# Gating and pooled products behind their pair's sixth product, the first output block out of its PSUM bank, SiLU as one ScalarE function

## The chip, the cores and the metric

The kernel runs on one core of one Trainium2 chip. The metric is device microseconds of one execution of the whole program, taken as the median of several runs; lower is better. A profile is one further execution, seen by the hardware profiler. Its engines are called PE (TensorE, the matmuls), DVE (VectorE), ACT (ScalarE), POOL (GpSimd) and SP (SyncE, which here issues most DMAs).

## The reference

One decoder layer on a sequence of 1024 tokens with 1024 channels, all in float32. One input projection feeds three token mixers and three gates:

```python
h = _rmsnorm(x, norm_g)
p = h @ w_in
(u, v, z_a, x_b, b_g, c_g, z_b, x_c, z_c, g_a, g_b, g_c) = jnp.split(p, ...)
# A: chunked spatial gating: u * (w_s . layernorm(gelu(v)) + b_s), u = gelu(u)
y_a = (_gmlp_branch(u, v, ln_g, ln_b, w_s, b_s) * jax.nn.silu(z_a)) @ w_pa
# B: gated causal convolution of width 3
y_b = (_shortconv_branch(x_b, b_g, c_g, conv_w, conv_b) * jax.nn.silu(z_b)) @ w_pb
# C: causal means over 2, 4, 8 or 16 tokens, minus x_c, times a 128 x 128 matrix per group
y_c = (_pool_branch(x_c, w_pool, pool_scale) * jax.nn.silu(z_c)) @ w_pc
merged = sigmoid(g_a) * y_a + sigmoid(g_b) * y_b + sigmoid(g_c) * y_c
out = _rmsnorm(x + merged @ w_o, final_g)
```

## The kernel before

**Stages.** First h is normalised, transposed and split into a high and a low half (a float32 product is made of three matmuls, `mm3`: high x high, high x low, low x high). v is projected by tokens and stored to DRAM. Then comes the long stage that the change touches, the input projection of everything else, and after it the branch projections (`py`, L699) and the output projection (`po`).

**Pairs.** The input projection walks over 28 `pairs` of 128-channel weight tiles (the loop at L497). Each pair has a kind: `g` (two gate tiles, Sigmoid), `a` (u and z_a), `b` and `bz` (the four tiles of mixer B), `c` (x_c and z_c). The first ten are g g g a g a g a g a; then b and bz take turns four times, then c and g four times, then two g. A pair's two output tiles, `o0` and `o1` (128 x 1024 each), are made by Strassen's scheme in Winograd's form: seven products of half size give four blocks. In the order of the code they are A11, A12, S2, S3, S1, A22, S4 (`PRODUCTS`, named by the left factor; PE rows in the profile carry these names). From the third pair on, A12's product is made for two neighbouring pairs together, ahead of the first of them, by cutting it once more into seven small products (`joint`); its result waits in SBUF as `p2`. So a pair then has six products of its own: A11, S2, S3, S1, A22, S4; A22 is the one that the title calls the sixth, S4 the last.

**Where a product goes.** Each product is one PSUM bank of 128 x 512 (`bank`, eight of them). ACT copies A11's to `s1`; DVE adds the others to running sums `u2` and `u3`, and `block` makes an output block of a bank and a sum and puts the pair's function on it. Weight tiles are combined on POOL (`T_n`, `T_j`), rounded on ACT (`ch`, `cj`) and their low halves made on DVE (`cl`), six products ahead (`AHEAD`).

**What an `a` pair adds.** In the `g` pair before it, `spatial` loads the mixer's weights and v (`vr`, 512 KB, from DRAM, on SP's queue) and `spatial_norm` normalises v: eight DVE instructions on `vr` (L425), two POOL multiplies and adds, an ACT rounding to `vh` and a DVE low half `vl`. `spatial_mm` (six matmuls into two banks, named `sg` in PE rows) is issued at the head of the `a` pair. The gating of the result (`gate`, by transposes `st`) is deferred as `late` into the next pair.

**What a `c` pair adds.** `pooled` makes windowed means on DVE, rounded to `ph` and `pw`; `pool_mm` (six matmuls, `pp`) is `late` too: it is issued in the next pair behind the fifth product, S1.

**Order and buffers.** The program is written once in this order; a scheduler then sets each engine's queue, and engines work strictly in the order of their queues. Tiles of one tag take turns in a fixed number of buffers: tag `m` has five of 128 x 1024, and `o0`, `o1`, `vr`, `vh`, `vl`, `st` all live there, so a tile's first write waits for the last reader of the tile whose buffer it gets.

Of the kernel before, what the change touches and what calls it, by code (L numbers as in the profile page):

```python
# [28 lines left out]

# Weight units, each [128, 1024] and contiguous in DRAM.  # L30
U_V = 0            # v: 4 units of 2 k-tiles x 512 columns
U_A = 4            # 4 channel tiles x (u, z_a): 8 k-tiles x 128 columns
U_B = 12           # 4 channel tiles x (c, x_b, b, z_b)
U_C = 28           # 4 channel tiles x (x_c, z_c)
U_G = 36           # 3 branches x 8 channel tiles
U_P = 60           # 3 branches x 4 units of 2 channel tiles (e, e + 4) x 4 k-tiles x 128
U_O = 72           # 8 k-tiles x 1024 columns
N_UNITS = 80

# h is cut into token halves x k halves (A11 .. A22), a pair of column tiles of  # L40
# the weights into k halves x tiles (B11 .. B22).  Seven products give the four
# output blocks (Strassen's scheme in Winograd's form):
#   S1 = A21 + A22   S2 = S1 - A11   S3 = A11 - A21   S4 = A12 - S2
#   T1 = B12 - B11   T2 = B22 - T1   T3 = B22 - B12   T4 = B21 - T2
PRODUCTS = (("A11", "B11"), ("A12", "B21"), ("S2", "T2"), ("S3", "T3"),
# [10 lines left out]
def hybrid_layer(ctx: ExitStack, tc: tile.TileContext, x, units, ws, wpool, small, rows, out):  # L56
# [32 lines left out]
    def rsqrt(src, scale, eps, at, dst=None):  # L89
        """(src * scale + eps) ** -0.5 = r * t: the reciprocal of the table's root and one Newton step."""  # L90
        a, r, t = (tmp[:, at[0], e, at[1]] for e in range(3))
        nc.vector.tensor_scalar(out=a, in0=src, scalar1=scale, scalar2=eps, op0=ALU.mult, op1=ALU.add)
        root = nc.scalar.activation(out=t, in_=a, func=AF.Sqrt)
        nc.vector.reciprocal(out=r, in_=t)
        tt(nc.vector, t, r, r, ALU.mult)
        tt(nc.vector, t, t, a, ALU.mult)
        nc.vector.tensor_scalar(out=t, in0=t, scalar1=-0.5, scalar2=1.5, op0=ALU.mult, op1=ALU.add)
        if dst is not None:
            tt(nc.vector, dst, r, t, ALU.mult)
        return root, r, t  # L100

    def gelu(x_, t, eng):
        """x * sigmoid(2c (x + 0.044715 x^3)), which is gelu's tanh form."""
        nc.scalar.activation(out=t, in_=x_, func=AF.Square)
        nc.vector.tensor_scalar(out=t, in0=t, scalar1=0.044715, scalar2=1.0, op0=ALU.mult, op1=ALU.add)
        tt(eng, t, t, x_, ALU.mult)
        nc.scalar.activation(out=t, in_=t, func=AF.Sigmoid, scale=GELU_SCALE)
        tt(eng, x_, x_, t, ALU.mult)

# [1 line left out]
    xs, rawv, wv = {}, {}, {}  # L111
# [35 lines left out]

# [1 line left out]
    norms = const.tile([P, 4, NT], F32, name="norms")  # L149
# [91 lines left out]

# [1 line left out]
    pairs = []  # L243
# [9 lines left out]
    for j in range(10, 12):  # L253
        pairs.append(("g", j, (U_G + 2 * j, U_G + 2 * j + 1)))
    # From the third pair on, the second product of two neighbouring pairs is taken
    # together and cut once more, the same way: token quarters x two k-tiles.
    steps = []
# [93 lines left out]
    def cut_again(first):  # L351
        """The quarters of A12 and their combinations; the last one takes A21's place."""
        hi, lo = hb["A12"]
        at = {"A11": (0, 0), "A12": (2, 0), "A21": (0, 256), "A22": (2, 256)}
        if first:
            f = {}
            for pr in (("A21", "A22"), ("A11", "A12")):
                t = slot("m", f"again_{pr[0]}", (P, 2, 2, 256))
                for e, name in enumerate(pr):
                    k0, c0 = at[name]  # L360
                    sub[name] = tuple(z[:, k0:k0 + 2, c0:c0 + 256] for z in (hi, lo))
                    f[name] = t[:, e]
                    tt(nc.vector, f[name], *(z.bitcast(F32) for z in sub[name]), ALU.add)
            for name, i0, i1, op in (("S1", "A21", "A22", ALU.add), ("S2", "S1", "A11", ALU.subtract),
                                     ("S3", "A11", "A21", ALU.subtract), ("S4", "A12", "S2", ALU.subtract)):
                f[name] = slot("q", f"again_{name}", (P, 2, 256)) if name in ("S1", "S2") else f["A21" if name == "S3" else "A12"]
                tt(nc.gpsimd, f[name], f[i0], f[i1], op)
                if name != "S4":
                    sub[name] = tuple(slot("wc", f"{name}{c}_again", (P, 2, 256), F32R) for c in "hl")
                    split_to(*sub[name], f[name])  # L370
            sub["f"] = f["S4"]
        else:
            sub["S4"] = sub["A21"]
            split_to(*sub["S4"], sub["f"])

    def joint(d0, d1):
        """The second product of two pairs, from their seven."""
        lo, hi = slice(0, 256), slice(256, HALF)
        nc.scalar.copy(out=d0[:, lo], in_=product())
        tt(nc.vector, d1[:, lo], product(), d0[:, lo], ALU.add)  # L380
        tt(nc.vector, d0[:, lo], product(), d0[:, lo], ALU.add)
        tt(nc.vector, d0[:, hi], product(), d1[:, lo], ALU.add)
        ps = product()
        tt(nc.vector, d1[:, hi], ps, d0[:, hi], ALU.add)
        tt(nc.vector, d1[:, lo], ps, d1[:, lo], ALU.add)
        tt(nc.vector, d0[:, hi], product(), d0[:, hi], ALU.add)
        tt(nc.vector, d1[:, lo], product(), d1[:, lo], ALU.add)

    # v of all tokens, then the first weights
    pend = []  # L390
# [14 lines left out]

# [1 line left out]
    def spatial(j):  # L407
# [43 lines left out]

# [1 line left out]
    wpt = {}  # L453
# [41 lines left out]
    late = None  # L495
    sp = None
    for p, (kind, j, _) in enumerate(pairs):  # L497
        nxt = pairs[p + 1] if p + 1 < len(pairs) else (None, None)
        if kind == "a":
            st = spatial_mm(j, *sp)  # L500
        f0, f1 = FUNCS[kind]
# [3 lines left out]
        def block(o, half, ps, part, func):  # L505
            dst = o[:, half]
            tt(nc.vector, dst, ps, part, ALU.add)
            if func == AF.Silu:
                sg = slot("q", f"sg{p}_{half.start}", (P, HALF))
                nc.scalar.activation(out=sg, in_=dst, func=AF.Sigmoid)  # L510
                tt(nc.gpsimd, dst, dst, sg, ALU.mult)
            elif func == AF.Gelu_apprx_tanh:
                gelu(dst, slot("q", f"sg{p}_{half.start}", (P, HALF)), nc.gpsimd)
            elif func:
                nc.scalar.activation(out=dst, in_=dst, func=func)  # L515
# [8 lines left out]
        u3 = slot("q", f"u3_{p}", (P, HALF))  # L524
        nc.scalar.copy(out=s1, in_=product())
        if nxt[0] == "a":
            sp = spatial(nxt[1])
        block(o0, lohalf, product() if p < PLAIN else p2, s1, f0)
        if p == PLAIN - 1:
# [3 lines left out]
        if nxt[0] == "a":  # L533
            sp = spatial_norm(nxt[1], *sp)
        if p == 0:
            cut_again(True)
        ps = product()
        if late is not None:
            late()
            late = None  # L540
        block(o1, hihalf, ps, u3, f1)
        tt(nc.vector, u2, ps, u2, ALU.add)
        block(o0, hihalf, product(), u3, f0)
        if kind == "g":
# [27 lines left out]

# [1 line left out]
    raws_p, wps = {}, {}  # L574
# [25 lines left out]

    # The output projection takes the same seven products: tokens of two tiles x
    # halves of k on the left, halves of k x halves of the columns on the right.
    right, staged, quad = {}, {}, {}
# [43 lines left out]
    def prep_left(t, r, ks):  # L647
        """One combination of merged for the tokens of tiles 2t and 2t + 1."""
        name = PRODUCTS[r][0]
# [62 lines left out]

# [1 line left out]
    while rights < 28:  # L714
# [20 lines left out]
    for t in range(PAIRS):  # L735
# [21 lines left out]
        def finish(i, q, c0, c1, psum_in, also=None):  # L757
            """One block of the residual stream and its squares."""
            o, acc = res[i][:, c0:c1], norms[:, q, i:i + 1]
# [73 lines left out]
def _layout(x, norm_g, w_in, ln_g, ln_b, w_s, b_s, conv_w, conv_b, w_pool,  # L833
            pool_scale, w_pa, w_pb, w_pc, w_o, final_g):
    """The inputs as the program reads them: moved, not changed."""
    import numpy as np
# [51 lines left out]
```

## Time and profile before

| | |
|---|---|
| median of 3 runs | 875.99 us (875.69 to 876.91) |
| span of the profiled execution | 873.6 us |
| median less that span | 2.4 us |
| PE busy in the span | 823.9 us |
| DVE busy | 722.2 us |
| POOL busy | 522.4 us |
| ACT busy | 345.2 us |

The profile lists no time of its own for the profiled execution beyond its span, which runs from the first to the last instruction; the runs' median lies 2.4 us above it. A busy time is a sum over stages with different limits. PE rows are pipelined: each lasts about 0.39 us on paper while the next one starts 0.23 us after it, so a distance in time is best read from start to start.

### The profile page before, as it was taken

Reading aid. Unit: us, or ns where it says so; the run is one execution under the profiler, and the core shown is the slowest. Engines: PE = TensorE matmul, PEld = TensorE weight load, DVE = VectorE, ACT = ScalarE, POOL = GpSimd, SP = SyncE. Lnnn points to the kernel's source line nnn. Section 1 sums busy time; section 2 is a strip of 40 time slices with the busy share of each in tenths; the row PEclk is TensorE's granted clock in tenths of the full one; section 3 lists DMA queues with packets and bytes.
Section 4 is the critical chain, followed back from the end, with each engine's and each line's share of the span. In section 5 each row is a group of like instructions: output and inputs, shape, how many; then the busy total and the mean of one; then the engine's idle time right before and its main releaser. Section 6 shows DMA issues by size and latency. Waiting matters only on the chain.

```text
span 873.6 us, 11272 instructions
## 1 busy us (share of the span) xinstructions
PE 823.9 (94%) x3886; PEld 689.0 (79%) x3886; DVE 722.2 (83%) x1077; ACT 345.2 (40%) x698; POOL 522.4 (60%) x411
## 2 busy tenths in 40 slices
PE   7979999989898999999999999999999999997991
PEld 6767788868686888888888888888888888785881
DVE  6995998989898889889899798989665826897995
ACT  4454845444443433333234443434452401444441
POOL 5667767878787867676676447374000353548743
PEclk9989999999999999999999999999999999999996
DMA  8110453141413122121312412222497543411142
GB/s 319 68 37 0 157 170 133 61 144 61 145 61 121 48 73 74 49 100 40 103 49 76 149 73 100 97 99 101 165 340 287 179 163 117 147 69 49 50 168 97
DMA packets 33593, 99.06 MB, mean 113 GB/s; under 512 B 3456, under 2 KB 9600, under 8 KB 33536
## 3 DMA queue, kind: packets, MB, share of 16 engines
q1 hardware_dynamic: 27920, 83.90, 27.7%
q10 hardware_dynamic: 5616, 14.44, 4.3%
q8 instruction: 31, 0.51, 0.2%
q14 instruction: 26, 0.21, 0.1%
HBM read 73.16 MB, written 25.17 MB: 113 GB/s over the span
## 4 chain that ended last, share of the span: by engine, by line
PE 64%; DVE 15%; POOL 10%; issue 6%; DMA 2%; ACT 2%; DVEq 0%; POOLq 0%; ACTq 0%
PE p L85 17%; PE p L84 17%; PE p L83 17%; PE py L699 10%; DVE al L76 3%; POOL T_n L76 3%; POOL o L76 2%; DVE tmp L76 2%; DVE rq L76 1%; POOL vr L76 1%; DMA rawo<-in_units_dram 1%; POOL S_a L76 1%; POOL T_o L76 1%; DVE mg L76 1%; DVE res L76 1%
## 5 line engine op out<-in xcount | busy, mean ns | idle before, releaser
L76 POOL TENSOR_TENSOR T_n<-raw,T_n 128x512 f32<-128x512 f32 x56 | 82.9, 1480 | 122.9 <-DVE cl L76 71.0
L76 DVE TENSOR_TENSOR cl<-T_n,ch 128x512 fp32r<-128x512 f32 x112 | 114.1, 1025 | 19.6 <-ACT ch L79 14.2
L79 ACT CAST ch<-T_n 128x512 fp32r<-128x512 f32 x112 | 69.3, 621 | 130.3 <-POOL T_n L76 73.7
L76 DVE TENSOR_TENSOR cl<-raw,ch 128x512 fp32r<-128x512 f32 x71 | 96.6, 1369 | 14.2 <-ACT ch L79 12.5
L76 DVE TENSOR_TENSOR o<-p,u 128x512 f32<-128x512 f32 x84 | 57.2, 681 | 16.7 <-PE p L85 16.7
L76 POOL TENSOR_TENSOR o<-o,sg 128x512 f32<-128x512 f32 x32 | 51.1, 1596 | 14.0 <-ACT sg L510 9.6
L79 ACT CAST ch<-raw 128x512 fp32r<-128x512 f32 x71 | 43.5, 619 | 36.1 <-PE p L84 34.5
L515 ACT ACTIVATE o<-o 128x512 f32<-128x512 f32 x48 | 30.3, 632 | 48.4 <-DVE o L76 43.2
L76 POOL TENSOR_TENSOR T_n<-raw,raw 128x512 f32<-128x512 f32 x28 | 46.4, 1658 | 1.1 <-DVE cl L76 0.6
L76 POOL TENSOR_TENSOR T_o<-rawo 128x512 f32<-128x512 f32 x4 | 7.1, 1770 | 65.1 <-DMA rawo<-in_units_dram 64.5
L83 PE MATMUL p<-A11h,ch 128*128 128x512 f32 x112 | 45.7, 408 | 0.0
L84 PE MATMUL p<-A11l,ch 128*128 128x512 f32 x112 | 45.7, 408 | 0.0
L85 PE MATMUL p<-A11h,cl 128*128 128x512 f32 x112 | 45.5, 406 | 0.0
L76 POOL TENSOR_TENSOR T_n<-raw 128x512 f32<-128x512 f32 x28 | 45.4, 1622 | 0.0
L83 PE MATMUL p<-S2h,ch 128*128 128x512 f32 x112 | 43.7, 390 | 1.0 <-ACT ch L79 1.0
L85 PE MATMUL p<-S4h,cl 128*128 128x512 f32 x112 | 43.7, 390 | 0.9 <-DVE cl L76 0.9
L85 PE MATMUL p<-S2h,cl 128*128 128x512 f32 x112 | 43.7, 390 | 0.4 <-DVE cl L76 0.4
L83 PE MATMUL p<-A22h,ch 128*128 128x512 f32 x112 | 44.0, 393 | 0.0
L85 PE MATMUL p<-S3h,cl 128*128 128x512 f32 x112 | 43.7, 390 | 0.1
L84 PE MATMUL p<-A22l,ch 128*128 128x512 f32 x112 | 43.6, 390 | 0.0
L85 PE MATMUL p<-A22h,cl 128*128 128x512 f32 x112 | 43.6, 389 | 0.0
L83 PE MATMUL p<-S3h,ch 128*128 128x512 f32 x112 | 43.6, 389 | 0.0
(470 smaller groups left out, 2667.9 us busy)
## 6 DMA issues: line engine op xcount, KB each, us to landing
raw<-in_units_dram SPq DMA_DIRECT2D x56, 512.0 KB, 3.3
gate<-o ACTq DMA_DIRECT2D x24, 512.0 KB, 3.3
gt<-gate SPq DMA_DIRECT2D x24, 512.0 KB, 4.2
rawp<-in_units_dram SPq DMA_DIRECT2D x12, 512.0 KB, 3.9
yr<-y SPq DMA_DIRECT2D x12, 512.0 KB, 4.3
x<-in_x_dram SPq DMA_DIRECT2D x8, 512.0 KB, 5.7
y<-o SPq DMA_DIRECT2D x8, 512.0 KB, 3.2
rawo<-in_units_dram SPq DMA_DIRECT2D x8, 512.0 KB, 3.4
```

Of the source, the lines that this page charges most:

```text
L76: eng.tensor_tensor(out=o, in0=a, in1=b, op=op)
L79: nc.scalar.copy(out=hi, in_=src)
L83: nc.tensor.matmul(ps, lhsT=wh, rhs=bh, start=first, stop=False)
L84: nc.tensor.matmul(ps, lhsT=wh, rhs=bl, start=False, stop=False)
L85: nc.tensor.matmul(ps, lhsT=wl, rhs=bh, start=False, stop=last)
L515: nc.scalar.activation(out=dst, in_=dst, func=func)
L699: nc.tensor.matmul(py[h], lhsT=w[:, tsl(c)], rhs=yt[b][h][s][:, c, :], start=c == 0 and w is wh and s == 0, stop=c == CT - 1 and w is wl)
```

## The change

Five things change in the loop over the pairs. `spatial_mm` moves from the head of its `a` pair to behind A22's product, and so does `late` (the gating of the `a` pair before, or the pooled product of the `c` pair before), which stood ahead of A22's blocks. The pair's first output block is added from A11's PSUM bank and `p2`, where it was added from `s1` and `p2`, both in SBUF. For kinds `bz` and `c`, SiLU is one ACT function in place of a Sigmoid on ACT and a multiply on POOL; kind `a` keeps the two. Comments are removed, which moves line numbers (Silu is L507 after, Sigmoid L515).

```diff
-        if kind == "a":
-            st = spatial_mm(j, *sp)
...
-            if func == AF.Silu:
+            if func == AF.Silu and kind != "a":
+                nc.scalar.activation(out=dst, in_=dst, func=func)
+            elif func == AF.Silu:
                 sg = slot("q", f"sg{p}_{half.start}", (P, HALF))
                 nc.scalar.activation(out=sg, in_=dst, func=AF.Sigmoid)
                 tt(nc.gpsimd, dst, dst, sg, ALU.mult)
...
-        nc.scalar.copy(out=s1, in_=product())
+        ps = product()
+        nc.scalar.copy(out=s1, in_=ps)
...
-        block(o0, lohalf, product() if p < PLAIN else p2, s1, f0)
+        if p < PLAIN:
+            block(o0, lohalf, product(), s1, f0)
+        else:
+            block(o0, lohalf, ps, p2, f0)
...
         ps = product()
-        if late is not None:
-            late()
-            late = None
         block(o1, hihalf, ps, u3, f1)
         tt(nc.vector, u2, ps, u2, ALU.add)
         block(o0, hihalf, product(), u3, f0)
+        if kind == "a":
+            st = spatial_mm(j, *sp)
+        sp = sp_next
+        if late is not None:
+            late()
+            late = None
```

PE's queue at the first `a` pair, before: the `sg` matmuls stand between S4 of the pair before and A11 of the pair.

```order
494 L85 MATMUL p_1368<-S4h,cl_1218 128x512
495 L83 MATMUL sg_0_1385<-vh_1318,wss_1257 128x512
496 L83 MATMUL sg_1_1390<-vh_1318,wss_1257 128x512
497 L83 MATMUL p_1404<-A11h,ch_1232 128x512
498 L84 MATMUL p_1404<-A11l,ch_1232 128x512
499 L85 MATMUL p_1404<-A11h,cl_1233 128x512
500 L84 MATMUL sg_0_1385<-vl_1319,wss_1257 128x512
501 L85 MATMUL sg_0_1385<-vh_1318,wss_1257 128x512
502 L84 MATMUL sg_1_1390<-vl_1319,wss_1257 128x512
```

The same products in PE's queue after:

```order
554 L85 MATMUL p_1476<-A22h,cl_1345 128x512
555 L83 MATMUL sg_0_1497<-vh_1318,wss_1257 128x512
556 L84 MATMUL sg_0_1497<-vl_1319,wss_1257 128x512
557 L85 MATMUL sg_0_1497<-vh_1318,wss_1257 128x512
558 L83 MATMUL sg_1_1502<-vh_1318,wss_1257 128x512
559 L84 MATMUL sg_1_1502<-vl_1319,wss_1257 128x512
560 L85 MATMUL sg_1_1502<-vh_1318,wss_1257 128x512
561 L83 MATMUL p_1511<-S4h,ch_1364 128x512
```

They moved five products back, to between A22 and S4.

DVE's queue around the blocks of A22 (`o_5_1806<-p_1898`) and S4 (`o_5_1807<-p_1922`) of the second `a` pair, before; `vr_2071` is v for the third `a` pair, `p_7` and `p_6` the small products of the next joint:

```order
245 L425 TENSOR_SCALAR vr_2071<-vr_2071,mv,lr 128x128
246 L76 TENSOR_TENSOR o_5_1806<-p_1898,u_5_1810 128x512
247 L425 TENSOR_SCALAR vr_2071<-vr_2071,mv,lr 128x128 x7
248 L105 TENSOR_SCALAR sg_512_1912<-sg_512_1912 128x512
249 L76 TENSOR_TENSOR cl_1974<-T_n_1971,ch_1973 128x512
250 L76 TENSOR_TENSOR o_5_1807<-p_1922,u_5_1809 128x512
```

The same stretch of DVE's queue after:

```order
246 L76 TENSOR_TENSOR o_5_1795<-p_1887,u_5_1799 128x512
247 L105 TENSOR_SCALAR sg_512_1901<-sg_512_1901 128x512
248 L425 TENSOR_SCALAR vr_2071<-vr_2071,mv,lr 128x128
249 L76 TENSOR_TENSOR cl_1974<-T_n_1971,ch_1973 128x512
250 L425 TENSOR_SCALAR vr_2071<-vr_2071,mv,lr 128x128 x2
251 L76 TENSOR_TENSOR o_5_1796<-p_1922,u_5_1798 128x512
252 L425 TENSOR_SCALAR vr_2071<-vr_2071,mv,lr 128x128 x5
```

The `vr` instructions now stand behind A22's block, and three of them ahead of S4's. In the built program the load of `vr` itself waits, for all of the second to fourth `a` pair, for the last `sg` matmul of the `a` pair before (before the change that was so for the third and fourth).

ACT's queue in the second `c` pair and the `g` pair after it, before (`sg<-o` is the Sigmoid of z_c, L515 the gates' Sigmoid):

```order
400 L510 ACTIVATE sg_512_4744<-o_20_4561 128x512
401 L79 CAST ch_4750<-T_n_4748 128x512
402 L79 CAST ch_4768<-raw_4579 128x512
403 L510 ACTIVATE sg_0_4786<-o_20_4561 128x512
...
410 L79 CAST cj_4900<-T_j_4832 128x256
411 L515 ACTIVATE o_21_4807<-o_21_4807 128x512
```

ACT's queue there after:

```order
406 L507 ACT_TABLE_LOAD
407 L507 ACTIVATE o_20_4541<-o_20_4541 128x512
408 L79 CAST ch_4728<-T_n_4726 128x512
409 L79 CAST ch_4746<-raw_4559 128x512
410 L507 ACTIVATE o_20_4541<-o_20_4541 128x512
...
416 L79 CAST cj_4865<-T_j_4808 128x256
417 L515 ACT_TABLE_LOAD
418 L515 ACTIVATE o_21_4783<-o_21_4783 128x512
```

A table load now stands ahead of each change between Silu and Sigmoid: eight in the whole program that were not there before, and 16 POOL multiplies fewer.

## Rows read from the trace of the kernel before

**Rows 1.** PE's waits of the whole span: microseconds in total, times, longest.

```profile
PE sg L83 <- ACT vh L79: 8.7, 3, 3.0
...
PE pp L83 <- ACT ph L79: 1.3, 1, 1.3
```

**Rows 2.** Busy time by stretch: PE, PEld, DVE, ACT, POOL, then clock, DMA share, GB/s.

```profile
97.50:139.90 42.40, 41.53 (x204) 35.00 (x203) 41.79 (x67) 22.66 (x40) 27.21 (x18) 1.00 0.38 130
139.90:183.00 43.10, 40.35 (x202) 34.03 (x201) 37.65 (x55) 19.82 (x37) 35.00 (x25) 1.00 0.34 115
183.00:227.86 44.86, 41.90 (x200) 35.10 (x201) 39.77 (x54) 19.02 (x36) 34.50 (x24) 0.96 0.29 101
227.86:272.75 44.89, 41.91 (x200) 35.10 (x201) 39.75 (x54) 19.01 (x36) 34.49 (x24) 0.96 0.30 100
272.75:310.00 37.25, 37.25 (x181) 31.62 (x182) 32.27 (x41) 16.43 (x31) 26.23 (x19) 0.95 0.20 72
310.00:350.00 40.00, 40.00 (x198) 33.97 (x197) 36.06 (x47) 12.64 (x24) 26.93 (x19) 1.00 0.24 79
```

**Rows 3.** PE in order of time, second a pair's head: start us, us, instruction.

```profile
179.86 0.39 PE L85 MATMUL p<-S4h,cl 128*128 128x512 f32 x1
183.00 0.74 PE L83 MATMUL sg<-vh,wss 128*128 128x512 f32 x2 [2.75 <-ACT vh L79]
...
184.95 0.63 PE L85 MATMUL p<-A11h,cl 128*128 128x512 f32 x1
...
187.92 0.40 PE L83 MATMUL p<-S2h,ch 128*128 128x512 f32 x1
```

**Rows 4.** PE and ACT in order of time, the last pooled product.

```profile
593.18 0.39 PE L85 MATMUL p<-S1h,cl 128*128 128x512 f32 x1
594.82 0.73 PE L83 MATMUL pp<-ph,wp 128*128 128x512 f32 x2 [1.25 <-ACT ph L79]
...
593.72 1.04 ACT L79 CAST ph<-pl 128x1024 fp32r<-128x1024 f32 x1 [2.35 <-issue]
```

**Rows 5.** PE, DVE and SP in order of time, second a pair.

```profile
189.97 0.39 PE L85 MATMUL sg<-vh,wss 128*128 128x512 f32 x1
190.39 0.53 SPq L420 DMA_DIRECT2D vr<-v_dram  x1
...
197.00 0.39 PE L83 MATMUL p<-A22h,ch 128*128 128x512 f32 x1
199.72 0.39 PE L83 MATMUL p<-S4h,ch 128*128 128x512 f32 x1
202.44 0.28 PE L83 MATMUL p<-A12h,ch 128*128 128x256 f32 x1
207.47 0.40 PE L83 MATMUL p<-A11h,ch 128*128 128x512 f32 x1
...
201.25 0.34 DVE L425 TENSOR_SCALAR vr<-vr,mv,lr 128x128 f32<-128x128 f32 x1
201.51 0.68 DVE L76 TENSOR_TENSOR o<-p,u 128x512 f32<-128x512 f32 x1
```

**Rows 6.** The tile vr: time from issue of its load to landing.

```profile
DMA to landing us min/median/max: 4.2/4.6/5.4
```

**Rows 7.** DVE by shape, 183 to 227.86 us: count, then busy us, mean ns.

```profile
L76 DVE TENSOR_TENSOR cl<-T_n,ch 128x512 fp32r<-128x512 f32 x8 | 9.5, 1209 | 1.2 <-ACT ch L79 1.2
L76 DVE TENSOR_TENSOR o<-p,s 128x512 f32<-128x512 f32 x2 | 2.5, 1230 | 0.0
```

**Rows 8.** ACT in order of time around a table load.

```profile
105.13 0.62 ACT L79 CAST A12h<-again_A 128x512 fp32r<-128x512 f32 x1
105.77 1.28 ACT L515 ACT_TABLE_LOAD   x1
107.06 0.63 ACT L515 ACTIVATE o<-o 128x512 f32<-128x512 f32 x1
```

**Rows 9.** ACT by line, whole span: busy us, mean ns, then idle before and its cause.

```profile
L515 ACT ACTIVATE o<-o 128x512 f32<-128x512 f32 x48 | 30.3, 632 | 48.4 <-DVE o L76 43.2 <-DMA wsr<-in_rows_dram 3.7 <-ACT ch L79 1.0
```

More of the change, by code (lines that the diff above doesn't have):

```diff
@@ L495, in hybrid_layer @@
     late = None
-    sp = None
+    sp = sp_next = None
     for p, (kind, j, _) in enumerate(pairs):
         nxt = pairs[p + 1] if p + 1 < len(pairs) else (None, None)
-        if kind == "a":
-            st = spatial_mm(j, *sp)
         f0, f1 = FUNCS[kind]
@@ L524, in hybrid_layer @@
         u3 = slot("q", f"u3_{p}", (P, HALF))
-        nc.scalar.copy(out=s1, in_=product())
+        ps = product()
+        nc.scalar.copy(out=s1, in_=ps)
         if nxt[0] == "a":
-            sp = spatial(nxt[1])
-        block(o0, lohalf, product() if p < PLAIN else p2, s1, f0)
+            sp_next = spatial(nxt[1])
+        if p < PLAIN:
+            block(o0, lohalf, product(), s1, f0)
+        else:
+            block(o0, lohalf, ps, p2, f0)
         if p == PLAIN - 1:
@@ L533, in hybrid_layer @@
         if nxt[0] == "a":
-            sp = spatial_norm(nxt[1], *sp)
+            sp_next = spatial_norm(nxt[1], *sp_next)
         if p == 0:
@@ L537, in hybrid_layer @@
         ps = product()
+        block(o1, hihalf, ps, u3, f1)
+        tt(nc.vector, u2, ps, u2, ALU.add)
+        block(o0, hihalf, product(), u3, f0)
+        if kind == "a":
+            st = spatial_mm(j, *sp)
+        sp = sp_next
         if late is not None:
@@ L540, in hybrid_layer @@
             late = None
-        block(o1, hihalf, ps, u3, f1)
-        tt(nc.vector, u2, ps, u2, ALU.add)
-        block(o0, hihalf, product(), u3, f0)
         if kind == "g":
```

## The prediction

> **What bounds the kernel now.** I read the list of what PE waited for first, since PE is busy 94% of the span. In the input projection it holds one wait that repeats, three times, 8.7 us in all: the `sg` matmuls waiting for ACT's `vh`; and one single wait of a pooled product for `ph` [rows 1]. Then I read the busy times by stretch. Of PE's 40.00 us none is idle in a stretch of the `b` and `bz` pairs, while DVE is busy 36.06 there, ACT 12.64 and POOL 26.93 [rows 2]: there PE alone sets the time, and what the change takes off DVE, ACT or POOL is worth nothing. In the `a` pairs it is another picture: the three periods from one `sg` to the next last 43.10, 44.86 and 44.89 us, and the clock's mean is 0.96 in two of them and 0.95 behind the third [rows 2]. The order of time shows why. `sg` starts 3.14 us after the last matmul of S4, where the distance is 0.23 otherwise, so 2.91 us are lost; and soon after it PE's starts stand further apart: from 184.95 to 187.92 us there are seven steps, 0.424 us each against 0.227 [rows 3]. That is the 1.2 GHz level instead of 2.4, granted right after an idle spell.
>
> **The spatial products' wait goes.** I take the loss apart by period. The idle times at the three places are 2.75, 2.96 and 2.98 us in the trace; with 0.16 us each that the pipelined end hides (2.91 less 2.75) they are 2.91, 3.12 and 3.14, together 9.2 us. The slow clock costs eight steps of 0.2 us each time, 1.6 us, three times 4.8. As a check, 43.10 less 2.91 is 40.2, and 44.86 less 3.12 less 1.6 is 40.1: the three periods agree on about 40.1 us as what PE itself needs. The `sg` matmuls move behind A22's product, five products of 2.72 us (197.00 to 199.72) [rows 5], so 13.6 us later. They came 2.9 to 3.1 us too early for `vh`, and `vl`, of 1.8 us, follows it; so they have some 9 us in hand, and the wait and its slow clock go: **14.0 us**.
>
> **The pooled product's wait goes.** `pp` started at 594.82 where PE could have had it at 593.41, so 1.41 us are lost; no slow steps follow. One product later PE comes 2.72 us later, and `ph` was ready at 594.76 [rows 4]: 1.3 us in hand. **1.4 us.**
>
> **What is late next: the load of v.** The load of `vr` now waits for the `sg` matmuls of the pair before, which are 13.6 us later. Before, it was issued at 190.39, right behind the last `sg` matmul, and landed some 4.6 us on (4.2 to 5.4) [rows 5, 6], well ahead of its first DVE instruction at 201.25. I count from the end of A22's product. `sg` takes six steps of 0.227, 1.36 us; S4 then 2.72 and the joint products 5.03 (202.44 to 207.47) [rows 5]; so the next A11 starts at 9.11 us. The load is issued at 1.55 and lands at 6.15 (5.75 to 6.95). DVE reaches the first `vr` instruction earlier: A22's block ended 2.5 us after the product (202.19 less 199.72) [rows 5], and the Square on ACT and its DVE instruction bring it to about 3.5. So DVE waits 2.65 us, a wait that the kernel did not have. Behind it in DVE's queue stand one `cl` (1.21 us in the mean here [rows 7]; I take 0.68, a block's time, as its least), two more `vr` of 0.26 from start to start, and S4's block, 0.68 [rows 5]. S4's bank therefore comes free at 6.15 + 0.26 + 1.21 + 0.52 + 0.68 = 8.8 us, between 7.9 (early landing, short `cl`) and 9.6 (late landing, mean `cl`). The first product that needs that bank is A11, eight banks on, at 9.11. So this costs 0 to 0.5 us at each of three places. A wait this short has no slow clock behind it, as the one of 1.25 us shows [rows 4]. I take 0.4 us in all, since the middle value fits.
>
> **DVE's time in a period.** It is 39.77 us now [rows 2]. The first block out of PSUM saves two times 1.230 less 0.68 [rows 7, 5], 1.1 us: 38.7 in a period of 40.1. Adding the 2.65 us of waiting gives 41.3, more than a period; but as DVE falls behind, the load has landed by the time it gets there, and the wait shrinks by as much. DVE was busy 41.79 of 42.40 us in the stretch before the first `sg`, with only 0.87 us of PE idle [rows 2]; that is why I let it pass at nothing, with the rival below as the other end.
>
> **Silu and its table loads.** 16 multiplies leave POOL, which waits for others in these pairs: nothing. Eight table loads of 1.28 us come to ACT, 10.3 us. They stand directly ahead of a Sigmoid or Silu which waits for a DVE sum (43.2 us of idle before 48 of them [rows 9]), so a load mostly fills idle time; behind it are `ch` casts for products several steps ahead, and ACT is busy 12.64 of 40 us. Nothing, and at most the whole 10.3 if that cover were gone. In the trace a load starts 0.02 us after the instruction ahead of it ends, and the Sigmoid 0.01 us after the load [rows 8], so the price is 1.28 and no more. The Trainium skill (ScalarE: Activation LUTs, What ACT_TABLE_LOAD costs) has about 1380 ns of drain on top, 2.66 us for every switch. The drain does not show in this trace; with it, and with every switch on the path, the sum would be 21.3 us worse instead of 10.3, and so above the time before.
>
> **The sum.** 14.0 + 1.4 - 0.4 = 15.0 us. In the profiled execution it is 873.6 to 858.6 of span. The runs' median lies 2.4 above that span, and I carry that over: 875.99 to **861.0 us**. Between 310 us and the branch projections PE has no other wait than that of `pp`, and the queues from the branch projections on are the same rows in the same order, so what is won is not lost on the way.
>
> **The rivals.** A difference below 0.2% (1.75 us) could not be told from no change.
> - *VectorE becomes the bound in the `a` pairs.* For it: 38.7 of 40.1 us, and POOL's 34.5 us are pressed into a shorter period (86% of it, 77% now), while a DVE instruction with both inputs in SBUF takes up to twice as long here (`cl` 1.21 against 0.68). If `cl` and its like grow in that proportion DVE has about 1.2 us more, 39.9. If also the 2.65 us of waiting don't shrink, a period takes 42.5, 2.4 more than PE needs, three times: 868 us. Against: PSUM's eight banks and six products ahead let DVE trail for several us, and only three periods are concerned.
> - *The table loads lie on the path.* 860.6 plus up to 10.3: 866 at half of them, 871 at all. Against: the idle time ahead of the Sigmoids, and rows 8.
> - *The load of v takes the place of the wait removed, and the kernel is slower.* Its place is A11 of the pair after each `a` pair but the last; each us of landing beyond some 5 is a us of PE, with 1.6 of slow clock once it is long. To lose all 15.4 the three places must cost 5.1 each, a landing at 8.5 us or more after issue. With 10 us it is 4.5 + 1.6 at each, three times, 879 us. Against: 4.2 to 5.4 in four loads. What could stretch it is another load ahead of it on SP's queue that waits.
> - *The time is given back further on.* The last stage waits for DMAs and DVE, and its end could be set by something that doesn't move with PE: then 873 to 876. Against: those loads are issued as buffers come free, which moves with PE.
>
> **How the numbers follow.** My forecast (859.3 to 863) 64%; VectorE 20%; table loads 5%; slower through the load of v 6%; given back 5%. The first three are faster by over 0.2%: 89%; the same 5%; slower 6%. The range goes from 859.3, a little below the sum with no new wait (860.6), up to 868.0, where VectorE's case ends; the upper half of the table loads' case and the last two are outside.
>
> **What would show it.** Right: no idle of PE before `sg` and `pp`, the clock at 1.00 from 140 to 840 us, periods of 40.1 us between `sg` groups, waits of DVE for the load of `vr` of up to 2.7 us, eight more table loads. Wrong: PE idle before A11 or within the joint products, by a bank or a `cl`; periods of 42 us; ACT's `ch` late behind a table load; or an end of the span that doesn't move with the branch projections.

## The result, and the profile after

| | before | changed |
|---|---|---|
| median of 4 runs each, us | 876.45 (875.69 to 876.92) | 863.00 (862.27 to 863.70) |
| ratio on record, 95% interval (the two medians alone give 0.985) | | 0.9858 [0.9840, 0.9875] |
| span of the profiled execution, us | 873.6 | 860.7 |
| start of the first `py` matmul, us | 639.5 | 627.6 |

The kernel became 1.4% faster: 861.0 were forecast, and 863.0 is the upper edge of the forecast's own 859.3 to 863; the stated range goes on to 868.0. Up to the branch projections it won 11.9 us, in the whole span 12.9; the sum had promised 15.0.

The waits of PE in the changed kernel (total us, times, longest) have neither `sg` nor `pp` any more [rows 1]. In their place stands one that was allowed 0.4 us:

```profile
PE p L83 <- DVE o L76: 3.4, 2, 2.1
```

Busy time by stretch, from one `sg` group to the next, and one stretch of the `b` and `bz` pairs (columns as in [rows 2]):

```profile
113.94:153.95 40.01, 40.01 (x197) 33.95 (x197) 36.92 (x56) 18.36 (x34) 28.41 (x20) 1.00 0.35 122
153.95:193.92 39.97, 39.97 (x201) 34.02 (x200) 35.24 (x49) 17.68 (x33) 28.47 (x20) 1.00 0.33 113
193.92:235.51 41.59, 40.25 (x202) 34.08 (x200) 39.51 (x53) 17.93 (x34) 32.90 (x22) 1.00 0.31 108
235.51:277.81 42.30, 40.24 (x202) 34.07 (x200) 39.70 (x53) 18.25 (x35) 33.14 (x22) 1.00 0.31 107
310.00:350.00 40.00, 40.00 (x198) 33.98 (x197) 34.99 (x47) 13.60 (x26) 26.08 (x16) 1.00 0.21 73
```

Where [rows 2] had three periods of 43 to 45 us, the clock at 0.96 in two of them, the clock is now 1.00 in all of these stretches; the first two are at what PE needs, 40.0, and the other two are 1.6 and 2.3 us longer. (It does not stay there up to 840 us, as the prediction had it: in the output projection PE waits 1.88 us for ACT's `ah`, and from 787.6 to 792.6 us the mean clock is 0.66. The kernel before has that wait too, 1.89 us, with a clock of 1.00 behind it.) In the two longer stretches PE stands still at A11:

```profile
204.53 0.50 PE L83 MATMUL p<-A11h,ch 128*128 128x512 f32 x1 [1.34 <-DVE o L76]
...
246.84 0.50 PE L83 MATMUL p<-A11h,ch 128*128 128x512 f32 x1 [2.06 <-DVE o L76]
```

A11 needs the bank of S4, eight banks back, and waits for the block that empties it. DVE in order of time shows why that block is late (start us, us, instruction; the idle time ahead of it in brackets), first where PE did not wait, then where it did:

```profile
155.09 0.68 DVE L76 TENSOR_TENSOR o<-p,u 128x512 f32<-128x512 f32 x1
156.53 0.43 DVE L105 TENSOR_SCALAR sg<-sg 128x512 f32<-128x512 f32 x1 [0.76 <-ACT sg L104]
159.50 0.95 DVE L425 TENSOR_SCALAR vr<-vr,mv,lr 128x128 f32<-128x128 f32 x1 [2.54 <-DMA vr<-v_dram]
160.37 0.68 DVE L76 TENSOR_TENSOR cl<-T_n,ch 128x512 fp32r<-128x512 f32 x1
160.97 0.59 DVE L425 TENSOR_SCALAR vr<-vr,mv,lr 128x128 f32<-128x128 f32 x2
161.48 0.68 DVE L76 TENSOR_TENSOR o<-p,u 128x512 f32<-128x512 f32 x1
...
196.86 1.77 DVE L76 TENSOR_TENSOR cl<-raw,ch 128x512 fp32r<-128x512 f32 x1
198.56 0.68 DVE L76 TENSOR_TENSOR o<-p,u 128x512 f32<-128x512 f32 x1
199.94 0.43 DVE L105 TENSOR_SCALAR sg<-sg 128x512 f32<-128x512 f32 x1 [0.70 <-ACT sg L104]
200.28 0.34 DVE L425 TENSOR_SCALAR vr<-vr,mv,lr 128x128 f32<-128x128 f32 x1
200.53 1.78 DVE L76 TENSOR_TENSOR cl<-T_n,ch 128x512 fp32r<-128x512 f32 x1
202.24 1.64 DVE L425 TENSOR_SCALAR vr<-vr,mv,lr 128x128 f32<-128x128 f32 x2
203.80 0.68 DVE L76 TENSOR_TENSOR o<-p,u 128x512 f32<-128x512 f32 x1
```

At the first place DVE does wait for the load of v, 2.54 us as forecast (2.65), and the bank is free at 162.16, 8.2 us after A22's end at 153.95: no wait of PE. At the second there is no wait for the load at all. DVE reaches `vr` 6.36 us after A22's end (193.92), close to the 6.15 that the landing had been given; but one `cl` and two `vr` then take 3.4 us instead of 1.3, and the bank is free at 204.48, after 10.56. What runs beside them is gelu on POOL (same columns; the first line is gelu at the first place, the second a SiLU multiply at the second):

```profile
159.06 1.30 POOL L76 TENSOR_TENSOR o<-o,sg 128x512 f32<-128x512 f32 x1 [0.74 <-ACT sg L107]
198.05 1.75 POOL L76 TENSOR_TENSOR o<-o,sg 128x512 f32<-128x512 f32 x1
200.45 1.32 POOL L76 TENSOR_TENSOR sg<-sg,o 128x512 f32<-128x512 f32 x1 [0.65 <-DVE sg L105]
202.51 1.28 POOL L76 TENSOR_TENSOR o<-o,sg 128x512 f32<-128x512 f32 x1 [0.74 <-ACT sg L107]
```

At the first place those two multiplies ran at 157.03 and 159.06, most of the time while DVE waited for the load. The second lasted to 160.36: the first `vr`, beside it, took 0.95 us instead of 0.34, and `cl`, behind it, 0.68. In the kernel before, `vr` stood ahead of gelu's instruction L105 in DVE's queue, and POOL was idle meanwhile; now it stands behind it. Before, at the second `a` pair:

```profile
202.11 1.87 DVE L425 TENSOR_SCALAR vr<-vr,mv,lr 128x128 f32<-128x128 f32 x7
203.90 0.42 DVE L105 TENSOR_SCALAR sg<-sg 128x512 f32<-128x512 f32 x1
204.40 1.68 POOL L76 TENSOR_TENSOR sg<-sg,o 128x512 f32<-128x512 f32 x1 [3.62 <-DVE sg L105]
```

The third place is the second over again, 0.7 us later (`vr` at 242.60, bank free at 246.79, 11.3 us after A22's end).

### The profile page after: what moved, and what is told of

Its sections match the earlier page's. It is cut to its first block, busy times and chain, and to the rows that moved or that the text cites. A ratio compares the mean times of both kernels' runs of the same rounds, so it can differ in the third digit from the quotient of the medians.

```text
span 860.7 us, 11286 instructions
## 1 busy us (share of the span) xinstructions
PE 820.5 (95%) x3886; PEld 687.6 (80%) x3886; DVE 705.1 (82%) x1077; ACT 355.6 (41%) x706; POOL 483.5 (56%) x395
## 4 chain that ended last, share of the span: by engine, by line
PE 72%; DVE 13%; POOL 5%; issue 4%; ACT 3%; DMA 2%; DVEq 0%; POOLq 0%; ACTq 0%
PE p L85 18%; PE p L83 18%; PE p L84 18%; PE py L706 10%; DVE rq L76 2%; PE po L83 2%; PE po L85 2%; PE po L84 2%; POOL T_n L76 1%; DVE mg L76 1%; DVE al L76 1%; DVE gt L76 1%; POOL S_a L76 1%; DVE tmp L76 1%; DVE x L168 1%
## 5 line engine op out<-in xcount | busy, mean ns | idle before, releaser
L76 DVE TENSOR_TENSOR cl<-T_n,ch 128x512 fp32r<-128x512 f32 x112 | 118.2, 1062 | 22.6 <-ACT ch L79 11.9
L76 DVE TENSOR_TENSOR cl<-raw,ch 128x512 fp32r<-128x512 f32 x71 | 83.5, 1188 | 9.9 <-ACT ch L79 7.2
L76 POOL TENSOR_TENSOR T_n<-raw,raw 128x512 f32<-128x512 f32 x28 | 43.5, 1552 | 5.9 <-DVE cl L76 4.4
L83 PE MATMUL p<-S4h,ch 128*128 128x512 f32 x112 | 43.9, 392 | 0.0
L84 PE MATMUL p<-A11l,ch 128*128 128x512 f32 x112 | 43.7, 390 | 0.0
L85 PE MATMUL p<-A11h,cl 128*128 128x512 f32 x112 | 43.6, 389 | 0.0
L84 PE MATMUL p<-S4l,ch 128*128 128x512 f32 x112 | 43.6, 389 | 0.0
L84 PE MATMUL p<-S2l,ch 128*128 128x512 f32 x112 | 43.6, 389 | 0.0
L84 PE MATMUL p<-S3l,ch 128*128 128x512 f32 x112 | 43.6, 389 | 0.0
L85 PE MATMUL p<-S1h,cl 128*128 128x512 f32 x112 | 43.6, 389 | 0.0
```

Source lines behind the costliest of these rows:

```text
L76: eng.tensor_tensor(out=o, in0=a, in1=b, op=op)
L83: nc.tensor.matmul(ps, lhsT=wh, rhs=bh, start=first, stop=False)
L84: nc.tensor.matmul(ps, lhsT=wh, rhs=bl, start=False, stop=False)
L85: nc.tensor.matmul(ps, lhsT=wl, rhs=bh, start=False, stop=last)
```

## Experiments

Each version stands against the kernel before, measured beside it; its median was 875.4 for the moves alone, block and SiLU, SiLU as before, and `vr` held behind; 874.6 for both at the old place, `vr` on ACT, gelu from the table, and both together; 875.39 for the block alone, the pooled products alone, the old place with `vr` on ACT, and v's own buffer. It was 876.45 beside the changed kernel, so a difference of a microsecond or two between versions of different groups is read from the traces and not from the medians.

**The parts of the change.** First the moves alone: SiLU and the first block as before.

```diff
-            if func == AF.Silu and kind != "a":
-                nc.scalar.activation(out=dst, in_=dst, func=func)
-            elif func == AF.Silu:
+            if func == AF.Silu:
...
-            block(o0, lohalf, ps, p2, f0)
+            block(o0, lohalf, p2, s1, f0)
```

> Only the two moves (spatial products and gating or pooled products behind the sixth product); the first block is still added from SBUF and SiLU is still Sigmoid and a POOL multiply. My account: the moves hold all of the gain and the other two edits only relieve VectorE (1.1 us a period) and GpSimd. So about 863 to 866 us: no wait before sg and pp, and the waits at A11 (1.3 and 2.1 us in the changed kernel) the same or up to 1 us longer each. Rival, that the PSUM block or SiLU carries part of the gain by itself: 867 us or more.

Measured: 864.26 us, ratio 0.9875 [0.9858, 0.9892]. The waits at A11 are 1.70 and 2.52 us, and one slow spell of the clock follows the second. The moves are nearly all of the gain.

The other two edits without the moves (`late()` and `spatial_mm` back where the kernel before has them):

> The block out of PSUM and the one-function SiLU, without the moves. My account: the three waits of sg for vh stay, each within 1 us of what it was (3 us), since GpSimd's chain sets them, and the slow clock behind them too: 874 to 876.5 us. The stretch of the other pairs stays at 100% PE. Rival, that these edits shorten GpSimd's and VectorE's chain to vh: waits of 1.5 us or less and no slow clock, under 871 us.

Measured: 871.58 us, 0.9954 [0.9941, 0.9967]: 2.4 us under the expected range, and 0.6 over the rival's. The three waits for `vh` are 7.2 us in all (8.7 before), and the pooled product's wait is gone, without its move. Of these two, the first block out of PSUM alone:

> The kernel before with one edit of the change alone: the first output block added straight out of the first product's PSUM bank. This edit and the one SiLU function together gave 871.58 us without the moves, 4 us under the kernel before of those runs, where 1 us was expected. Theory 'SiLU as one function is worth nothing here as it was worth nothing beside the moves': 871 to 872.2, with the three waits for vh about 7.2 us in total and no wait of a pooled product. Rival 'the SiLU function took the pooled product's wait away, the bank edit shortened the waits for vh': 872.8 to 874, vh about 7.2 us and the pooled product's wait of 1.3 us still there.

Measured: 872.87 us, 0.9965 [0.9952, 0.9978]. PE's waits of that version:

```profile
PE sg L83 <- ACT vh L79: 6.9, 3, 2.5
...
PE pp L83 <- ACT ph L79: 1.3, 1, 1.3
```

The pooled product's wait is back, so it was SiLU as one function that had taken it: the rival holds, by its row and by its time. The bank edit alone shortens the waits for `vh` from 8.7 to 6.9. The two times differ by 1.3, about that wait, though their intervals overlap.

The changed kernel with SiLU as Sigmoid and a POOL multiply again:

> The changed kernel with SiLU as Sigmoid and POOL multiply again: eight table loads of 1.28 us fewer, 16 multiplies more. My account: the loads lie beside other work and GpSimd is not waited for in those pairs, so within 0.5 us of the changed kernel, 862.5 to 863.5 us. Rival, that table loads cost time on the path: 1 us or more faster than the changed kernel. Rival, that GpSimd's relief is worth something: 1 us or more slower.

Measured: 863.30 us, 0.9862 [0.9845, 0.9879], the same span as the changed kernel, 860.7. With the moves there, SiLU and its table loads are worth nothing either way.

**Which of the moves.** The line `late()` defers two things, the pooled products of a `c` pair and the gating of an `a` pair. Both back at their old place, behind the fifth product:

```diff
         ps = product()
+        if late is not None:
+            late()
+            late = None
         block(o1, hihalf, ps, u3, f1)
...
         sp = sp_next
-        if late is not None:
-            late()
-            late = None
```

> The changed kernel with the pooled products (and the transposes of the gating, which are issued by the same call) back ahead of the sixth product's additions, the spatial products left behind it. In the kernel before, TensorE waited 1.3 us once for a pooled product, and in the version with the bank and SiLU edits alone that wait was gone already. Theory 'moving the pooled products is worth nothing beside the other edits': 862.3 to 863.8, no wait of a pooled product for ScalarE above 0.3 us. Rival, as predicted: 1.4 us are lost again: 864 to 865.

Measured: 868.54 us, 0.9925 [0.9910, 0.9940]. Neither theory said so. No pooled product waits; what grew is the wait at A11, with a slow clock behind it:

```profile
206.40 0.80 PE L83 MATMUL p<-A11h,ch 128*128 128x512 f32 x1 [2.80 <-DVE o L76]
...
250.79 0.80 PE L83 MATMUL p<-A11h,ch 128*128 128x512 f32 x1 [2.81 <-DVE o L76]
```

ACT's queue differs in the gating pair: its two sigmoids for o1 now stand ahead of a weight's copy (ACT in order of time, this version):

```profile
187.11 0.64 ACT L515 ACTIVATE o<-o 128x512 f32<-128x512 f32 x1 [1.05 <-DVE o L76]
189.51 0.63 ACT L515 ACTIVATE o<-o 128x512 f32<-128x512 f32 x1 [1.76 <-DVE o L76]
190.05 0.60 ACT L79 CAST ch<-raw 128x512 fp32r<-128x512 f32 x1
190.56 0.58 ACT L526 COPY s<-p 128x512 f32<-128x512 f32 x1
```

The copy of A11's product to `s1` comes at 190.56; in the changed kernel it is at 187.74, ahead of the second sigmoid at 188.98. DVE waits for that weight's copy and is then 1.8 us later at the `a` pair (its `cl` behind A22 starts at 198.69 instead of 196.86). DVE in order of time, this version; in the changed kernel the same `cl` starts at 188.87 without a wait:

```profile
190.68 0.69 DVE L76 TENSOR_TENSOR cl<-raw,ch 128x512 fp32r<-128x512 f32 x1 [1.21 <-ACT ch L79]
```

With the pooled products alone moved back:

> The changed kernel with the pooled products alone back ahead of the sixth product's additions; the gating's transposes and products, which went back with them in the foregoing version and made it 868.54, stay behind. Theory 'moving the pooled products is worth nothing beside the other edits, and the 5 us of that version are the gating's': 862.3 to 863.8. Rival, as predicted: 1.4 us of the pooled product's wait are lost: 864 to 865.

Measured: 863.97 us, 0.9869 [0.9856, 0.9882], 0.2 over the theory's range and 0.03 under the rival's. The wait that the rival needs is not there: PE waits for no `ph`. What its two crowded periods have more than those of the changed kernel is a slow clock in one of them, behind a wait at A11 of the same length (2.07 us):

```profile
236.07:280.01 43.94, 41.87 (x202) 35.23 (x201) 41.86 (x55) 20.00 (x39) 34.63 (x23) 0.96 0.30 103
```

So of the second move, the gating is what counts here, by the difference of the two versions; the gating alone was not moved back.

**What makes the block late.** Held behind S4's block of the pair, the eight `vr` instructions leave the way to the bank free:

```diff
-        block(o1, lohalf, product(), u2, f1)
+        behind = block(o1, lohalf, product(), u2, f1)
...
-        for i in range(NT):
-            nc.vector.tensor_scalar(out=vr[:, i, :], ...)
+        with tc.issue_after(behind):
+            for i in range(NT):
+                nc.vector.tensor_scalar(out=vr[:, i, :], ...)
```

> The changed kernel with the eight normalising instructions of v held in VectorE's queue until behind the last product's block of the pair before, so that they no longer stand ahead of the block whose bank A11 needs. My account: that place in the queue, with cl and vr stretched beside GpSimd's multiply (1.7 us for one cl, 1.6 for two vr), makes the two new PE waits, so both go or shrink below 0.5 us: about 3 us faster than the changed kernel, 859.5 to 861 us. Rival, late landing of the load of v: the instructions still come when the load has landed, and the waits go too, but then they should reappear in the first period only. Rival, that VectorE has too much work in these pairs altogether: the waits move to the joint products or to a cl and the time stays within 1 us of 863.

Measured: 863.41 us, 0.9864 [0.9850, 0.9879]. No wait at A11; PE now waits at S3 for the bank of a joint product:

```profile
209.49 0.50 PE L83 MATMUL p<-S3h,ch 128*128 128x512 f32 x1 [0.53 <-DVE p L76]
...
252.21 0.50 PE L83 MATMUL p<-S3h,ch 128*128 128x512 f32 x1 [1.83 <-DVE p L76]
```

The last rival holds: the work is only moved, and the two periods last 40.81 and 42.69 us, together 83.5 as against 83.9. So the work itself was taken off DVE:

```diff
+    nc.vector.scalar_tensor_tensor(out=nb, in0=mv[:, :, 0], scalar=-1.0, in1=lr, op0=ALU.mult, op1=ALU.mult)
...
-            nc.vector.tensor_scalar(out=vr[:, i, :], ...)
+            nc.scalar.activation(out=vr[:, i, :], in_=vr[:, i, :], func=AF.Identity, scale=lr[:, i:i + 1], bias=nb[:, i:i + 1])
```

> The changed kernel with the eight normalisations of v before each spatial product (24 in the three crowded pairs, mean 569 ns on VectorE) done by ScalarE as Identity with scale and bias; one small VectorE product at the start makes the bias. Theory 'VectorE has too much work in the stretch from A22 to the next A11 of the branch A pairs': it loses about 4.2 us of its 39.6 us per pair, so the two waits of TensorE at A11 (1.34 and 2.06 us, and what the bank costs around them, 1.6 and 2.3 us of the stretches 41.59 and 42.30) go and no new one comes: 859 to 860. Rival 'the order of the queue, not the amount': with the normalisations off VectorE the waits would go as well, but ScalarE, which has 18 of 42 us of work there, would hand over vr later and other waits come: within 1 us of 863.

Measured: **858.76 us**, 0.9815 [0.9798, 0.9832], 0.24 under the theory's range. No wait at A11, and the crowded periods:

```profile
194.09:234.07 39.98, 39.98 (x201) 34.02 (x200) 34.40 (x45) 21.48 (x43) 33.86 (x22) 1.00 0.35 112
234.07:274.39 40.32, 40.26 (x201) 33.94 (x200) 34.38 (x45) 20.69 (x42) 33.51 (x23) 1.00 0.33 111
```

The other way, gelu from ACT's table, takes one small instruction (L105) from DVE and two multiplies from POOL in each of the pair's two halves:

```diff
-                gelu(dst, slot("q", f"sg{p}_{half.start}", (P, HALF)), nc.gpsimd)
+                nc.scalar.activation(out=dst, in_=dst, func=func)
```

> The changed kernel with gelu of branch A's first factor as one ScalarE function from the table (the same that v takes) in the place of square, scale, multiply, sigmoid, multiply: per half it takes two 128x512 multiplies from GpSimd (1.3 us each), one 0.43 us instruction from VectorE and one pass from ScalarE, and adds table loads on ScalarE (up to four per pair, 1.28 us each). Theory 'VectorE is stretched by GpSimd's multiplies that now run beside it' (a cl took 1.78 us beside them and 0.64 us alone): both waits at A11 fall under 0.5 us: 859 to 861. Rival 'VectorE's own amount of work': only 0.86 us per pair goes, so the waits fall by less than 1 us each: 861.5 to 863. If the table loads lie on the path it comes out above 863.5, with waits of VectorE for ScalarE at o or sg.

Measured: **858.84 us**, 0.9820 [0.9802, 0.9838], 0.16 under the theory's range, and no wait at A11. The chain to S4's block at the second place, `cl` and two `vr` among them, is short again (DVE in order of time), and the bank is free 7.7 us after A22's end at 193.86:

```profile
199.50 0.35 DVE L425 TENSOR_SCALAR vr<-vr,mv,lr 128x128 f32<-128x128 f32 x1 [1.66 <-DMA vr<-v_dram]
199.76 0.69 DVE L76 TENSOR_TENSOR cl<-T_n,ch 128x512 fp32r<-128x512 f32 x1
200.37 0.60 DVE L425 TENSOR_SCALAR vr<-vr,mv,lr 128x128 f32<-128x128 f32 x2
200.88 0.68 DVE L76 TENSOR_TENSOR o<-p,u 128x512 f32<-128x512 f32 x1
```

Busy time by stretch:

```profile
193.86:233.84 39.98, 39.98 (x201) 34.02 (x200) 34.77 (x52) 22.57 (x38) 28.51 (x19) 1.00 0.33 112
233.84:273.79 39.95, 39.95 (x201) 34.02 (x200) 34.79 (x52) 22.59 (x38) 28.51 (x19) 1.00 0.32 113
```

DVE by shape in the first of the two, in this version (count, then busy us, mean ns, then idle time before and its cause):

```profile
L425 DVE TENSOR_SCALAR vr<-vr,mv,lr 128x128 f32<-128x128 f32 x8 | 2.3, 341 | 1.7 <-DMA vr<-v_dram 1.7
L76 DVE TENSOR_TENSOR cj<-T_j,cj 128x256 fp32r<-128x256 f32 x5 | 1.9, 420 | 1.6 <-ACT cj L79 1.6
```

The same groups of the changed kernel, in 193.92 to 235.51:

```profile
L425 DVE TENSOR_SCALAR vr<-vr,mv,lr 128x128 f32<-128x128 f32 x8 | 4.3, 588 | 0.0
...
L76 DVE TENSOR_TENSOR cj<-T_j,cj 128x256 fp32r<-128x256 f32 x4 | 3.7, 963 | 0.0
```

DVE is busy 4.7 us less in the period (39.51 to 34.77), of which only 0.9 are the two instructions L105 that left (430 ns each). The rest is the same instructions, shorter: by the sums of their durations, which overlap a little, `vr` 2.0 less and `cj` 1.8 less with one more of them counted. That is the stretching beside POOL, measured. No wait of PE goes back to the 16 table loads that this version adds.

Both together:

> The changed kernel with both of the foregoing edits that unload VectorE and GpSimd: v's normalisation on ScalarE and gelu from ScalarE's table. If VectorE's lateness in the branch A pairs is all that is left there, it cannot be faster than with the normalisation alone: 859 to 860, the branch A pairs 40.0 us apart from one spatial product to the next. If ScalarE now becomes late (18 us of 42 busy before; some 3 us and up to four table loads of 1.28 us more, two passes of 0.6 us less): above 861, with TensorE waiting for ch or vh of ScalarE.

Measured: 859.71 us, 0.9826 [0.9809, 0.9844]. Not faster than either, as the theory said, and its periods are 40.6 and 40.9 us where the theory had 40.0, for ACT is now a little late: PE waits 0.9 us in two pieces for ACT's copy of a joint product. Ahead of that copy, behind the last `vr`, stands one of gelu's table loads; here it does lie on the path (ACT in order of time):

```profile
204.59 1.28 ACT L511 ACT_TABLE_LOAD   x1
...
206.42 0.35 ACT L379 COPY p<-p 128x256 f32<-128x256 f32 x1
```

The old place of gating and pooled products together with `vr` on ACT:

> The version with gating and pooled products back at their old place, and v's normalisation on ScalarE. Theory 'the old place of the gating puts the two sigmoids of a gate ahead of a weight's copy in ScalarE's queue, so VectorE comes 1.8 us later into the stretch that it fills anyway, and TensorE's waits at A11 grow': with 4 us per pair taken off VectorE that lateness is absorbed, and the time is that of the changed kernel with the same edit, 858.2 to 860. Rival 'the old place costs TensorE by itself': the 5 us stay, 863 to 865.

Measured: 863.03 us, 0.9862 [0.9849, 0.9874]. The theory falls in its second half: the lateness is not absorbed, and the time is the rival's, 4.3 us over that of `vr` on ACT alone. Still, what PE loses there is not lost by the place itself but in waits for ACT. DVE has room (35.27 us of 41.47 in the second period), but PE waits 2.6 us in two pieces for ACT, where five `vr` of the pair stand ahead of the copy that frees a joint product's bank (ACT in order of time):

```profile
203.87 2.03 ACT L427 ACTIVATE vr<-vr,nb,lr 128x128 f32<-128x128 f32 x5
205.80 0.61 ACT L511 ACTIVATE sg<-o 128x512 f32<-128x512 f32 x1
206.32 0.35 ACT L379 COPY p<-p 128x256 f32<-128x256 f32 x1
```

So whichever engine carries `vr` must not be late when it enters this stretch. That the order of ACT's queue is what makes it late is read from the traces; no version changed that order alone.

Last, a buffer of v's own, so that its load is not tied to the `sg` matmuls:

```diff
-    BUFS = {"h": 14, "wc": 18, "raw": 4, "T": 3, "q": 6, "m": 5}
+    BUFS = {"h": 14, "wc": 18, "raw": 4, "T": 3, "q": 6, "m": 5, "v": 1}
...
-        vr = slot("m", f"vr{j}", (P, NT, P))
+        vr = slot("v", f"vr{j}", (P, NT, P))
```

> The changed kernel with a buffer of its own for v's rows, so that their load does not wait for the buffer of the pair before and VectorE's eight normalisations stand a product or two earlier or later in its queue, mostly ahead of the stretch behind the sixth product. No work is removed. Theory 'what counts is how much VectorE has between A22 and the next A11, not in the whole pair': the waits at A11 go or fall under 0.5 us each: 859 to 861. Rival 'the amount in the whole pair counts', as the version with the normalisations held back suggested (863.41): the waits move elsewhere, 862 to 863.8.

Measured: 871.96 us, 0.9963 [0.9950, 0.9976], far over what either theory gives. One buffer still ties the load to the last reader of the v before (`vl`, done at 187.48): it is issued at 187.51, lands some 6.5 us later, and the `vr` instructions now stand so early in DVE's queue that everything waits behind them:

```profile
194.01 0.86 DVE L425 TENSOR_SCALAR vr<-vr,mv,lr 128x128 f32<-128x128 f32 x3 [2.88 <-DMA vr<-v_dram]
```

PE then waits at several places, for `o`, `u` and `st`, and a period takes 45.0 us. It says nothing on the two theories, since the wait came from the load; two buffers were not tried. Nor was L105 put back behind `vr`, which would test DVE's order by itself.

## Why the prediction came out as it did

**Spatial products: right.** No idle time before `sg`, and no slow clock around it; at the second place `vl` ends at 185.93, 8.0 us ahead of `sg`, where some 9 were forecast. Where nothing new takes its place the full amount shows: the first `py` starts 15.4 us earlier than before with `vr` on ACT (624.1) and 16.0 with gelu from the table (623.5), against 14.0 + 1.4.

**Pooled product: right, but not the move's alone.** The 1.4 us are gone, and the move does it by itself, as forecast; but SiLU as one function, put at nothing, takes that wait away too (beside the bank edit). The two edits share one gain. The `late()` move matters through the gating instead, which I had given no term: with both at the old place the time is 5.5 us longer.

**The new wait: the term that was mis-sized.** The place (A11, S4's bank), the chain (load of v, `vr`, `cl`, two `vr`, the block) are as written. The first transition fits by its total (8.2 us, forecast as 7.9 to 9.6), in part by luck: the load was there 0.6 us early and `cl` was 0.6 us short, the first `vr` 0.6 us long. The step that failed is "6.15 + 0.26 + 1.21 + 0.52 + 0.68 = 8.8 us". At the second place it measured 6.36 + 4.20 = 10.56, at the third 7.09 + 4.19 = 11.28. A11 is due at 9.11, so the bank came 1.45 and 2.17 us too late; with the way from bank to matmul and a longer first step, the periods (41.59 and 42.30 against 39.98 and 39.95 with gelu from the table) are 4.0 us longer in all, where 0.4 was forecast. The terms that were mis-sized are the two `vr`, 1.56 us for 0.52 from start to start, and the `cl`, 1.71 for 1.21; at the third place DVE also arrived 0.94 us late. The `vr` had been priced at rows in which POOL was idle beside them, the `cl` at a mean. The move put gelu's L105 ahead of `vr` in DVE's queue, and so POOL's multiplies beside `vr` and `cl`. The trace before held the warning: its one `vr` beside a POOL instruction (117.13, POOL from 116.20 to 118.36) took 1.31 us. 15.4 less 4.0 is 11.4, and 11.9 were measured at `py`.

**VectorE as the bound: half of it came.** The rival's mechanism, DVE's two-input instructions stretched beside a denser POOL, is what happened, at two of the three periods and with 41.6 and 42.3 us for its 42.5. Its chance of 20% was too low. It isn't the amount alone, though: DVE was idle for 2.1 and 2.6 us of these periods, yet late where a bank was waited for.

**SiLU and table loads: right in this kernel.** Nothing beside the moves (863.30 us without them). It is not so everywhere: without the moves SiLU takes the pooled product's wait, and with both gelu and `vr` on ACT a table load stands ahead of a copy that PE waits for.

**The end: 1.0 us that was not foreseen.** The gain grows from 11.9 at `py` to 12.9 at the end. From the first `py` on the kernel before takes 234.1 us and the changed one 233.1; the other versions, whose edits all lie ahead of `py`, take 232.4 to 234.0. So 1.0 us is within what this stretch varies by, and nothing shows it to be the change's. In the chain that ended last, the load of the residual takes 4.50 us in the profile before and 3.58 here, 3.2 to 4.2 in the others.

## What to carry to other kernels

When a wait is removed by moving instructions, look at what else changes its neighbour in an in-order queue: the durations taken from the trace before hold only if the neighbour is as idle beside them as it was; here it was GpSimd beside VectorE. Before trusting a margin of a microsecond, look for the longest time that the trace shows for each instruction in the chain. And where two engines trail a bound one, taking work off either (normalisation to ScalarE, or gelu's multiplies off GpSimd) gave some 4 us more, while holding the same work back a little gave nothing.

## What the runs showed of the hardware

- A DVE instruction whose inputs lie in SBUF was stretched beside POOL, one that reads PSUM was not: `cl` took 0.68 us alone and 1.78 beside POOL's multiply, two `vr` 0.59 and 1.64; `o<-p,u` at 198.56 took 0.68, all of it within POOL's multiply of 198.05 to 199.80. The `cl` that started 0.08 us after POOL's multiply ended 0.54 us after it. The Trainium skill (SBUF — State Buffer, Who interferes with whom) says that the two engines' shared ports are held by one instruction to its end and the other blocks, for DVE instructions with two SBUF inputs and for `tensor_scalar` in its two-port mode; these rows agree with it. In which mode `vr`, a `tensor_scalar`, ran is shown by no row.
- The same wait had two outcomes at the clock: after 2.06 us of waiting at A11 the period of the changed kernel has a granted clock of 1.00, as has the version with SiLU as before after 2.07 us; after 2.07 us in the version with the pooled products moved back it has 0.96, the 1.2 GHz level for a while, and is 1.64 us longer (43.94 against 42.30). The wait of 1.88 us in the output projection, above, is another such pair.
- A table load in the crowded pairs took 1.28 us and its neighbour started 0.01 us later, as in [rows 8]; what it costs is what waits behind it (ACT, gelu from the table):

```profile
193.72 1.28 ACT L510 ACT_TABLE_LOAD   x1
195.01 0.63 ACT L510 ACTIVATE sg<-o 128x512 f32<-128x512 f32 x1
```
